# RMSNorm and matmul on one core: the stores of tiles 0 and 1 divided into eleven transfers each

## The chip, the cores and the metric

The kernel runs on one core of one Trainium2 chip. The metric is the device time of one execution in microseconds (us); lower is better. The kernel before takes 209.87 us, the median of three runs (209.15 to 210.03). A profile is one execution recorded by the hardware profiler. In it PE is TensorE's matmul, PEld its weight load, DVE VectorE, ACT ScalarE, POOL GpSimd and SP SyncE, which computes nothing and only issues transfers. Sixteen DMA engines move the data; a transfer (one `dma_start`) is cut into packets that are spread over them, and each engine that takes part reports its part's end to a semaphore.

## The reference

```python
# x: 16 x 1024 x 512, gamma: 512, weight: 512 x 768, all float32; eps = 1e-5
rms = np.sqrt(np.mean(x ** 2, axis=-1, keepdims=True) + eps)
x_norm = x / rms * gamma
return np.matmul(x_norm, weight).astype(np.float32)
```

There are 16,384 tokens. The input x is 33.6 MB and the output 50.3 MB; with the weights of 1.6 MB all of it crosses between HBM and the core's memory once.

## The kernel before, in words

**Tiles.** A tile is 128 tokens, one on each partition; there are 128 tiles, worked on in pairs (2j, 2j+1). For each tile ACT squares and sums the 512 features (`square`, L205), and from the sums come the root (L210, ACT) and its reciprocal `rstd` (L212, DVE). POOL casts x to bf16 (`cast`, L188). TensorE turns the tile so that features lie on partitions (`transpose_word`, L239; DVE copies the result from PSUM, L248). One quad of tiles in sixteen is cast at L269 and turned by DVE instead (L280). TensorE then multiplies by the weights, which gamma has already scaled: four weight loads (L305) and eight products (L309) per tile into one of three accumulators. `finish_tile` scales the accumulator by `rstd` and writes it to the output tile `ot`: even tiles by ACT (L288), odd tiles by DVE (L290). Then it calls `store`.

**Loads.** `load` (L177) brings x in stretches of 4 tiles (twice) and then of 8. Those of tiles 0 to 31 and the two halves of the weights (L354) are issued by SP at the very start; later ones by ACT, each when the loop reaches a set pair (`load_until`). Gamma (L349) is the first transfer of all: two rows of 1024 bytes, issued by ACT.

**Stores.** `store` (L297 to L302) does nothing until the last tile of a stretch is written, and then issues one transfer for the whole stretch on SP. The stretches (`o_first`, `o_size`, L138) are 1, 1, 2 and 4 tiles in the first group, 8 tiles in each of the middle groups, and 4, 4, 4, 2, 2 at the end: 22 stores. The output tiles lie in three buffers of 8 tiles; group g writes buffer g % 3. So tiles 24 to 31 write the buffer from which tiles 0 to 7 were stored, and have to wait until those stores have landed. In general, ACT's and DVE's writes of group g wait for the stores of group g - 3.

**Rows.** `rows` (L140) says which rows of x or of the output belong to a tile. In the first eight tiles, a stretch of 4 tiles takes 512 tokens in a row, and partition p holds tokens 4p to 4p + 3. The store of tile 0 alone (or of tile 1 alone) therefore writes 128 separate rows of 768 floats, 3072 bytes each. A store of 8 tiles writes 24,576 bytes together from each partition.

**Order.** Nothing is scheduled by a planner. The code calls `run` and `order.transfer` in the order that is wanted, and `Order.emit` (L39 to L97) issues the instructions to each engine in that order. It finds from the cells that each step reads and writes which earlier steps it has to wait for, and puts those waits ahead of it on its engine. A transfer is a step of its own with its own semaphore, or one whose last transfer is known to be done; whoever waits for a transfer waits for that semaphore. An engine runs its instructions in order, so a wait holds up all that is queued behind it on that engine. SP's queue has, in order: the early loads, and then the 22 stores.

Of the kernel before, what the change touches and what calls it, by code (L numbers as in the profile page):

```python
# [16 lines left out]
P = 128  # L17
# [83 lines left out]
def kernel(  # L101
# [9 lines left out]
    PE, DVE, ACT, POOL, SP = nc.tensor, nc.vector, nc.scalar, nc.gpsimd, nc.sync  # L111
    order = Order(tc)
# [5 lines left out]
    out = out.flatten_outer_dims()  # L118
# [5 lines left out]
    XG, OG = 16, 8  # L124
# [15 lines left out]
    def rows(ap, i, n):  # L140
        base, t = (i - i % OG, OG) if OG <= i < XG else (x_first[i], x_size[i]) if i < OG else (i - i % XG, XG) if i < 2 * XG else (i - i % (2 * XG), 2 * XG)
        return ap[base * P:(base + t) * P, :].rearrange("(p t) d -> p t d", t=t)[:, i - base:i - base + n, :]

    def sb(name, shape, dtype):
        return nc.alloc_sbuf_tensor(name, shape, dtype).ap()
# [14 lines left out]
    ot = [sb(f"ot{n}", [P, OG, O], F32) for n in range(3)]  # L160
# [7 lines left out]
    def cells(name, slot, i, n=1):  # L168
        return [(name, slot, t) for t in range(i, i + n)]
# [124 lines left out]
    def accumulator():  # L294
        return next(turns) % 3

    def store(i):  # L297
        first, n = o_first[i], o_size[i]
        s = first // OG % 3
        if i == first + n - 1:  # L300
            src = ot[s][:, first % OG:first % OG + n, :]
            order.transfer(SP, lambda: SP.dma_start(out=rows(out, first, n), in_=src), reads=cells("ot", s, first % OG, n))  # L302

    def hold(lhsT, of):
        run(PE, lambda: PE.ldweights(lhsT), of)  # L305
# [20 lines left out]
    def finish_tile(i, a, engine):  # L326
        s = i // OG % 3

        before = [("ot", s, i % OG - 1)] if i == o_first[i] + o_size[i] - 1 else []
        scale(engine, ot[s][:, i % OG, :], ops[a][:, :O], rstd[:, i:i + 1],  # L330
              [("ops", a, 0), ("ops", a, 1), ("rstd", i)] + before, [("ot", s, i % OG)])
        store(i)
# [158 lines left out]
```

## Time and profile before

| | |
|---|---|
| median of three runs | 209.87 us (209.15 to 210.03) |
| profiled execution: its own time | 208.59 us |
| its span (first to last instruction) | 206.6 us |
| busy in the span | PE 193.4, PEld 72.6, DVE 149.5, ACT 144.3, POOL 59.9 us |
| moved | 85.62 MB in 5920 packets, mean 414 GB/s |
| the two stores of 384 KB | 20.5 us from issue to landing (median) |
| DMA packets under 512 bytes | 658 |

How to read it: the span is less than the time of the execution, since the time holds what lies before the first and after the last instruction. Busy times say how long each engine was at work, not what the end waited for. That is read from the chain of waits (followed back from the last instruction to whatever released it), from stages of the span (busy time and DMA share in each) and from the landings of transfers. A DMA share of 1.00 means that all sixteen engines were moving packets all of the time. A transfer's time to landing counts from its issue, so it holds the time that it stood in line behind others.

### The profile page before, as it was taken

The numbers are of one execution on the slowest core, as the hardware profiler recorded it, in microseconds if no ns is written. First come the engines' busy times: TensorE is split into PE (matmuls) and PEld (weight loads), VectorE is DVE, ScalarE is ACT, GpSimd is POOL, SyncE is SP. The second block draws the span as 40 slices with busy tenths as digits, with TensorE's granted clock in tenths as the row PEclk, the third lists the DMA queues.
The fourth block names the chain that finished last, engine by engine and source line by source line (L and its number), as shares of the span: only waits on it lengthen the run. The fifth ranks groups of instructions, "written<-read, shape, count | busy, mean of one in ns | idle before, by whom it ended". The sixth has DMA issues, their size and how long they took to land.

```text
span 206.6 us, 2755 instructions
## 1 busy us (share of the span) xinstructions
PE 193.4 (94%) x1212; PEld 72.6 (35%) x717; DVE 149.5 (72%) x255; ACT 144.3 (70%) x343; POOL 59.9 (29%) x34
## 2 busy tenths in 40 slices
PE   6699999999999999999999999999999999999940
PEld 0134444433334333433333333433344324343310
DVE  0446556999579975999569974999569974999530
ACT  2698998777777687677877687676948758683310
POOL 1436752067005250063304242060703307000000
PEclk9799999999999999999999999999999999999995
DMA  5999999999999999999999999999999999999993
GB/s 207 428 444 425 412 388 423 423 441 425 433 428 425 428 438 427 424 430 425 431 438 425 425 433 417 443 424 424 428 425 438 433 428 428 436 424 405 416 418 165
DMA packets 5920, 85.62 MB, mean 414 GB/s; under 512 B 658, under 2 KB 660, under 8 KB 1556
## 3 DMA queue, kind: packets, MB, share of 16 engines
q1 hardware_dynamic: 4176, 60.29, 69.0%
q10 hardware_dynamic: 1732, 25.17, 28.7%
q8 instruction: 7, 0.11, 0.2%
q14 instruction: 5, 0.04, 0.0%
HBM read 35.13 MB, written 50.33 MB: 414 GB/s over the span
## 4 chain that ended last, share of the span: by engine, by line
PE 75%; DMA 15%; DVE 5%; issue 1%; ACT 1%; SPq 0%; ACTq 0%
PE ps L309 66%; DMA out_dram<-ot 12%; PE ps L239 9%; DMA xt<-in_x_dram 2%; DVE ot L290 2%; DVE xT L248 1%; DVE xTq L280 1%; ACT ot L288 0%; ACT jk L205 0%; DVE w_bf L290 0%; DVE rstd L212 0%; ACT rms L210 0%; SPq L486 0%; ACTq L93 0%; SPq L445 0%
## 5 line engine op out<-in xcount | busy, mean ns | idle before, releaser
L309 PE MATMUL ps<-w_bf,xT 128*128 128x256 bf16 (+1 forms) x783 | 145.7, 326 | 1.8 <-DVE w_bf L290 0.5
L288 ACT ACTIVATE ot<-ps,rstd 128x768 f32<-128x768 f32 x64 | 57.5, 898 | 47.4 <-PE ps L309 38.0
L188 POOL CAST xb<-xt 128x2048 bf16<-128x2048 f32 (+3 forms) x21 | 46.4, 2218 | 113.3 <-PE ps L239 57.4
L205 ACT ACTIVATE w_f<-xt 128x512 bf16<-128x512 f32 x124 | 76.3, 619 | 0.1
L290 DVE TENSOR_SCALAR ot<-ps,rstd 128x768 f32<-128x768 f32 x64 | 64.8, 1013 | 10.3 <-PE ps L309 9.3
L305 PEld LDWEIGHTS <-xT 128*128 128x128 bf16 x400 | 39.4, 98 | 60.4 <-issue 59.1
L239 PE MATMUL ps<-ident_f,xb 128*128 128x128 f32 x200 | 54.0, 273 | 1.7 <-POOL xb L188 1.6
L248 DVE COPY xT<-ps 128x1024 bf16<-128x1024 bf16 (+1 forms) x53 | 34.6, 654 | 24.3 <-PE ps L239 23.7
L280 DVE STREAM_TRANSPOSE xTq<-xq 32x256 f32<-32x256 f32 x112 | 48.7, 435 | 1.9
L239 PEld LDWEIGHTS ps<-ident_f,xb 128*128 128x128 f32 x200 | 28.1, 141 | 46.6 <-issue 43.8
L309 PE MATMUL ps<-w_bf,xTq 128*128 128x256 bf16 (+1 forms) x217 | 41.8, 324 | 0.4
L205 ACT ACTIVATION_READ_ACCUMULATOR w_f<-xt 128x1 f32 x124 | 23.6, 191 | 0.0
L305 PEld LDWEIGHTS <-xTq 128*128 128x128 bf16 x112 | 11.0, 98 | 14.5 <-issue 14.5
L269 POOL CAST xq<-xt 128x2048 bf16<-128x2048 f32 x7 | 13.3, 1893 | 0.0
L212 DVE RECIPROCAL rstd<-rms 128x8 f32<-128x8 f32 (+3 forms) x20 | 3.9, 193 | 8.9 <-ACT rms L210 8.7
L210 ACT ACTIVATE rms<-ssq,eps_sb 128x8 f32<-128x8 f32 (+3 forms) x20 | 6.0, 300 | 0.7
L309 PE MATMUL ps<-warm 128*128 128x512 bf16 x10 | 4.3, 568 | 1.4 <-DVE eps_sb L363 1.4
L205 ACT ACTIVATE jk<-xt 128x512 bf16<-128x512 f32 x4 | 2.5, 618 | 3.1 <-DMA xt<-in_x_dram 3.1
L288 ACT ACTIVATE w_bf<-w_f,g_sb 128x768 bf16<-128x768 f32 x2 | 1.9, 936 | 1.1 <-DMA w_f<-in_weight_dram 1.1
L386 DVE COPY g_sb<-ps 128x4 f32<-128x4 f32 x1 | 0.2, 161 | 3.1 <-PE ps L380 3.1
L350 ACT ACT_TABLE_LOAD x1 | 1.3, 1283 | 1.5 <-SPq L445 1.5
L290 DVE TENSOR_SCALAR w_bf<-w_f,g_sb 128x512 bf16<-128x512 f32 (+2 forms) x3 | 1.4, 481 | 0.6 <-DMA w_f<-in_weight_dram 0.6
(12 smaller groups left out, 3.0 us busy)
## 6 DMA issues: line engine op xcount, KB each, us to landing
out_dram<-ot SPq DMA_DIRECT2D x13, 3072.0 KB, 22.6
xt<-in_x_dram ACTq DMA_DIRECT2D x12, 2048.0 KB, 19.5
xt<-in_x_dram SPq DMA_DIRECT2D x3, 2048.0 KB, 17.7
out_dram<-ot SPq DMA_DIRECT2D x4, 1536.0 KB, 10.8
out_dram<-ot SPq DMA_DIRECT2D x3, 768.0 KB, 6.7
xt<-in_x_dram SPq DMA_DIRECT2D x2, 1024.0 KB, 6.9
w_f<-in_weight_dram SPq DMA_DIRECT2D x2, 768.0 KB, 7.1
out_dram<-ot SPq DMA_DIRECT2D x2, 384.0 KB, 20.5
```

Of the source, the lines that this page charges most:

```text
L188: run(POOL, lambda: POOL.tensor_copy(out=xb[s][:, i % 8:i % 8 + n, :], in_=src), of, cells("xb", s, i % 8, n))
L205: run(ACT, lambda: ACT.activation(out=dst, in_=src[:, 0, :], func=AF.Square, accum_out=ssq[:, i:i + 1]), of, to + [("ssq", i)])
L210: run(ACT, lambda: ACT.activation(out=rms[:, s], in_=ssq[:, s], func=AF.Sqrt, scale=1.0 / D, bias=eps_sb), [("ssq", t) for t in range(i, i ...
L212: run(DVE, lambda: DVE.reciprocal(out=rstd[:, s], in_=rms[:, s]), [("rms", i)], [("rstd", t) for t in range(i, i + n)])
L239: run(PE, lambda: PE.transpose(out=tp[b][:, t, h, :], in_=words[:, lo:lo + P], identity=ident_f), cells("xb", s, j % 4 * 2 + t) + ["ident" ...
L248: run(DVE, lambda: DVE.tensor_copy(out=dst[:, t:t + n, :], in_=src[:, t:t + n, :]), [("tp", b)], cells("xT", j % 4, t, n))
L269: run(POOL, lambda: POOL.tensor_copy(out=xq[s], in_=src), of, [("xq", s)])
L280: run(DVE, lambda: DVE.transpose(out=dst, in_=src), [("xq", s)], [("xTq", s, n)])
L288: run(ACT, lambda: ACT.mul(out=dst, in_=src, mul=r), reads, writes)
L290: run(DVE, lambda: DVE.tensor_single_scalar(out=dst, in_=src, scalar=r, op=mybir.AluOpType.mult), reads, writes)
L305: run(PE, lambda: PE.ldweights(lhsT), of)
L309: run(PE, lambda: PE.add_instruction(mybir.InstMatmult(name=nc.get_next_instruction_name(), engine=mybir.EngineType.PE, ins=[PE.lower_ap(r ...
```

## The change

The stores of tiles 0 and 1 are no longer one transfer each but eleven, all issued by SP, one after the other. Together they write the same 128 rows to the same places. The parts are cut by partition:

- eight transfers of seven rows: partitions 0, 4, ..., 24; then 1, 5, ..., 25; 2, ..., 26; 3, ..., 27; and the same four from 32 on (32, 36, ..., 56 and so on)
- one transfer of 64 rows: partitions 64 to 127
- two transfers of four rows: partitions 28 to 31, and 60 to 63

All other stores stay as they were. SP issues 42 stores in place of 22. Each of the new transfers has a semaphore, so ACT, before it writes tile 24, waits for eleven transfers of tile 0 instead of one, and DVE before tile 25 for eleven of tile 1. The order of the instructions on all engines but SP is unchanged.

```diff
+    DIVIDED = (0, 1)
+    PARTS = [slice(lo + m, lo + 28, 4) for lo in (0, 32) for m in range(4)] + [slice(64, P), slice(28, 32), slice(60, 64)]
+
     def store(i):
         first, n = o_first[i], o_size[i]
         s = first // OG % 3
         if i == first + n - 1:
-            src = ot[s][:, first % OG:first % OG + n, :]
-            order.transfer(SP, lambda: SP.dma_start(out=rows(out, first, n), in_=src), reads=cells("ot", s, first % OG, n))
+            src, dst = ot[s][:, first % OG:first % OG + n, :], rows(out, first, n)
+            for part in PARTS if first in DIVIDED else [slice(0, P)]:
+                store_rows(dst[part], src[part], cells("ot", s, first % OG, n))
+
+    def store_rows(dst, src, of):
+        order.transfer(SP, lambda: SP.dma_start(out=dst, in_=src), reads=of)
```

## The prediction

> **What bounds the kernel now.** I read the page first (engine and DMA rows in 40 slices), then stages, then the chain that ended last, then the stores, and last the packet and landing records of the trace.
>
> From the page, the slices (tenths busy, one column per 5.2 us):
>
> ```profile
> PE   6699999999999999999999999999999999999940
> ...
> DMA  5999999999999999999999999999999999999993
> GB/s 207 428 444 425 412 388 423 423 441 425 433 428 425 428 438 427 424 430 425 431 438 425 425 433 417 443 424 424 428 425 438 433 428 428 436 424 405 416 418 165
> ```
>
> TensorE and the sixteen DMA engines are both full from the third slice to the last but two. The stages part them (time in each stage, PE busy and instructions, then PEld, DVE, ACT, POOL, granted clock, DMA share, GB/s):
>
> ```profile
> 26.00:44.00 18.00, 17.89 (x119) 7.26 (x72) 13.47 (x23) 15.49 (x40) 6.91 (x3) 1.00 1.02 424
> 44.00:80.00 36.00, 35.74 (x230) 13.40 (x133) 29.15 (x49) 27.11 (x67) 11.48 (x6) 1.00 1.00 427
> ...
> 160.00:180.00 20.00, 19.42 (x125) 7.20 (x72) 15.25 (x27) 14.77 (x36) 5.51 (x3) 1.00 1.01 430
> 180.00:190.00 10.00, 9.95 (x66) 3.86 (x39) 9.65 (x18) 5.75 (x13) 0.00 (x0) 1.00 0.98 420
> 190.00:200.00 10.00, 8.60 (x53) 2.48 (x26) 5.67 (x8) 3.19 (x4) 0.00 (x0) 1.00 0.98 414
> 200.00:207.00 7.00, 0.00 (x0) 0.00 (x0) 0.00 (x0) 0.00 (x0) 0.00 (x0) 0.65 0.50 206
> ```
>
> From 44 us on the DMA share is 0.98 to 1.01 while TensorE already rests 1.40 us in 190:200. So the end belongs to transfers. The chain, its last long piece and who waits for a store:
>
> ```profile
> 142.42 25.11 DMA out_dram<-ot
> 167.62 0.91 ACT ot L288
> ...
> 198.69 1.02 DVE ot L290
> ```
>
> ```profile
> L302 SPq DMA_DIRECT2D out_dram<-ot x22: 332/332/348, 13.0 to 200.0; - x22
> ...
>   ACT ot L288: 9.2, 4
>   DVE ot L290: 0.4, 1
> ...
> DMA to landing us min/median/max: 5.7/22.0/25.4
> ```
>
> The last store is issued at 200.00 and lands 5.7 us later. The chain calls all that one DMA, but the landing records split it: each engine reports its own sixteenth. These are the sixteen landings of the last store (us), then the latest landing of each of the last six stores:
>
> ```
> 203.22 203.28 203.30 203.31 203.31 203.39 203.40 203.46 203.73 203.94 203.96 204.00 204.66 204.72 205.06 205.66
> 190.71 194.47 198.22 201.96 203.81 205.66
> ```
>
> The latest engine moves 98 KB (its part of 1536 KB) in 3.75 us and 49 KB in 1.85 us, back to back, to the end: it never runs dry, and its backlog, not the last tile, ends the kernel. Eight engines are through by 203.46, 2.20 us sooner. Every store before the change gives each engine the same bytes, so the lag comes from elsewhere: instruction packets (seven of 16 KB, near 1 us each), and slow packets (of the 1527 packets of 24576 bytes after 56 us, 1384 took 911 to 916 ns, and about a hundred 922 to 962). A change of the bytes per engine therefore moves the end one for one, if it touches the last engine.
>
> **The change part by part.** A tile's store is 128 rows of 3072 bytes: 16 engines with 8 rows each (the two stores left 256 packets of that size). A seven-row transfer can occupy at most seven engines, a four-row one four; 64 rows give four to each of sixteen. The nearest row for a short transfer is the gamma load: two rows, two packets, started 1 ns apart on two engines. Which engines the seven are, no row tells. One end: a different set each time, then the load stays near eight rows and nothing moves. Other end: always the same seven, and the four-row ones the first four of them. I take the second, since the five 128-row transfers of the first 22 us landed with the same spacing each time (0 to 0.46 us): the assignment is fixed, not turning. Then per tile four engines carry 8+4+2 = 14 rows, three 8+4 = 12, nine 4 in place of 8.
>
> The Trainium skill, DMA: Bandwidth & Descriptors (Why a DMA increments its semaphore by 16 and not by 1), states the same split: the largest count up to 16 that divides the rows, on the lowest-numbered engines; no run here shows the numbers.
>
> Prices: a 3072-byte packet took 121 ns (median of 256, mean 122, longest 229), a semaphore packet 9 ns. Over both tiles:
> - four engines: 12 x 121 + 20 more semaphore packets x 9 = +1.63 us
> - three engines: 8 x 121 + 16 x 9 = +1.11 us
> - nine engines: -8 x 121 = -0.97 us (none above -8 x 229 = -1.83).
>
> Issue on SP: 20 more at 0.33 us is 6.6 us (at most 1.25 us each, the longest issue of this trace, which is 25). The first store was issued at 12.95, the second at 14.49, the store of tiles 2 and 3 at 17.35, the next at 24.54. With the change the second starts near 16.8 and tiles 2 and 3 near 20.6, 3.2 us late. All is hidden: the same queue still holds x loads, and the first 3072-byte packet moved only at 26.05. If that cover went, the store of tiles 8 to 15 (36.36) would come late next. No load is queued behind on SP: later x loads are issued by ACT.
>
> Waits: ACT waits for eleven transfers instead of one before it writes tile 24, DVE the same before tile 25; queued behind are the squares of later tiles (ACT), and on DVE the transposes that TensorE's products need. The tiles' stores landed by 41.01, ACT writes tile 24 at 48.49, so with 1.63 us more they are still there; what is left is ten passed waits. None below zero; above, ten times the shortest short instructions (ACT's accumulator read, 191 ns) is 1.9 us on each. I take zero, because ACT sat idle 0.70 us for TensorE before that tile and 0.48 before the next, and DVE's queue is 29.15 of 36 us busy; a rest would eat TensorE's lead over the transfers (1.40 us idle in 190:200), not the end.
>
> Sum: the latest engine, if one of the nine, ends at 205.66 - 0.97 = 204.69; the other late ones likewise at 204.09 or before. The four heavier ones, if among the first twelve, end at 203.22 + 1.63 = 204.85 to 204.00 + 1.63 = 205.63. The end is the later: between 204.69 and 205.63, so -0.97 to -0.03; I take the middle of where the eight early ones put it (203.46 + 1.63 = 205.09) and a little above, 205.2, so -0.45 us. The profiled execution took 208.59 (span 206.6 and 2.0 around it), 1.28 under the median of the runs and under the fastest of them; the sum gives 208.14 for it and 209.87 - 0.45 = 209.4 for the median.
>
> Nine in sixteen engines being relieved, a late engine is one of them with 0.56 by count. Seven engines began their x packets early (1.96 to 2.04 us; one of gamma's two among them, the other one held by gamma to 2.97), eight late (2.69 to 2.83). As far as chains of packets, each starting where one ended, can be followed, six of the early seven are through by 203.6; if the short transfers sit on gamma's side, they load early engines, so I go to 0.65. The Trainium skill (same page, Latency and other measured facts) calls engines 7 and 15 usually the slower ones; by it the last engine is relieved here. No run here shows which number it has.
>
> **Rivals.**
> 1. Slower: a heavier engine was already late. From a landing later than 205.66 - 1.63 = 204.03 the load makes the end worse: 204.66 gives +0.63, 205.06 gives +1.03, 205.66 gives +1.63 (three engines' share: +1.11). For it: four landings lie above 204.03, and by count alone one of the four heavier engines is likelier than not to have one of them. Against: the early start group above. 210.5 to 211.5; +1.05 is passed only by the last engine itself or by the waits on top.
> 2. Slower: transfers of one row per engine cost more than their bytes. For it: in 26:35, where the two small stores moved, the rate was 410 GB/s against 427 in 44:80, 4% of 9 us, 0.36 us; eleven times the transfers gives up to 3.9 us, 213.8. It decides from (1.05 + 0.45) / 20 = 75 ns per extra transfer. Against: two 768 KB stores at the end took 2 x 1.85 us where one of 1536 KB took 3.75, so an additional boundary cost nothing. The Trainium skill (same page, Rules for kernel authors) says transfers under 64 KB pay mostly overhead, and these have 21 and 12 KB; no row here has such a store.
> 3. Same: the seven turn round the engines, or the heavier ones reach just the old end: 209.87.
> 4. Faster: the relieved engine gains more than its rows' median (up to 1.83 us, 208.0), and the heavier engines were idle at the end, waiting for the store issued at 200.00, so that their load costs less. For it: the early eight land together, as engines do that wait for an issue. Against: mean packet 122 ns.
>
> **How the numbers follow.** About 0.5% (1.05 us) is what a measurement here can tell from no change. Forecast 0.52, all of it within 0.5% (-0.97 to 0; its own range 208.9 to 209.9). Rival 1: 0.24, of it 0.16 slower by over 0.5%, 0.08 within. Rival 2: 0.12, slower. Rival 3: 0.03, within. Rival 4: 0.09, faster. Faster 0.09, same 0.63, slower 0.28. The range goes from 208.7 (a part of rival 4) to 211.5 (all of rival 1) and leaves out rival 2 and most of rival 4, under 0.2.
>
> **What would show it.** The landings of the small stores: seven-row ones with seven late parts. In the last store, the spread from first to last landing (2.44 us) shrinks to about 1.5 with the last one near 205.2. The chain still ends with the last store, issued within 0.3 us of 200.00. Rate in the slice around 26 to 35 us shows rival 2: a fall well under 410 GB/s. Wrong, if the spread grows (rival 1), if TensorE's busy share falls in the stage 44:80 (waits), or if the last store's fastest part lands clearly later than 203.22.

## The result, and the profile after

The changed kernel takes 211.14 us (median of six runs, 210.65 to 211.38). Beside it the kernel before took 209.81 us. The ratio is 1.0086, with a 95% interval of 1.006 to 1.0112: slower by 0.9%, where -0.2% was forecast. The ratio and its interval are formed from undisturbed executions alone, and are not the quotient of the two medians, which is 1.0063. 211.14 lies within the stated range, on its wrong side.

The profiled execution took 210.70 us with a span of 208.6, against 208.59 and 206.6. The page of the changed kernel, slices of 5.2 us (line numbers of the changed file are 7 higher behind the store: L316 is L309 of before, L309 is L302):

```profile
PE   7799999999999999998998989999898999999980
DMA  5999999999999999999999999999999999799886
GB/s 220 420 441 440 390 383 418 427 447 413 438 423 432 441 416 438 412 434 427 429 435 424 435 427 429 416 421 430 434 435 421 435 424 443 324 415 415 337 343 286
```

Before, the DMA row stood at 9 up to the last slice. Now the transfers thin out in the last sixth, and TensorE has gaps in the middle instead. The stages say the same:

```profile
44.00:80.00 36.00, 36.00 (x235) 13.42 (x134) 29.05 (x48) 26.86 (x65) 11.24 (x6) 1.00 1.01 430
80.00:120.00 40.00, 38.71 (x252) 14.77 (x146) 32.21 (x55) 28.14 (x68) 10.93 (x4) 1.00 1.01 430
120.00:160.00 40.00, 38.19 (x246) 14.22 (x141) 28.70 (x48) 26.04 (x63) 11.06 (x5) 1.00 1.00 426
160.00:180.00 20.00, 19.11 (x124) 7.07 (x71) 15.69 (x27) 16.35 (x39) 7.33 (x3) 1.00 1.01 431
180.00:190.00 10.00, 10.00 (x68) 4.04 (x40) 9.57 (x18) 7.44 (x20) 0.00 (x0) 1.00 0.88 374
190.00:200.00 10.00, 10.00 (x65) 3.24 (x33) 7.65 (x12) 3.61 (x4) 0.00 (x0) 1.00 0.79 332
```

TensorE rests 1.29 + 1.81 + 0.89 us in the stages from 80 to 180, in all 4.0; before it was 0.26 + 0.26 + 0.58 = 1.1 (39.74 of 40 twice, 19.42 of 20). After 180 TensorE is full, and the DMA share falls to 0.79. The kernel before ended on transfers with TensorE at rest; this one ends on TensorE with engines of the DMA at rest. What TensorE waited for is told by the list of waits (us in all, times, longest), before and after; then come the store's view and the chain from 90 us on, both after:

```profile
ACT ot L288 <- DMA out_dram<-ot: 9.2, 4, 2.7
...
DVE ot L290 <- DMA out_dram<-ot: 0.4, 1, 0.4
PE ps L309 <- ACT ot L288: 0.4, 1, 0.4
```

```profile
ACT ot L288 <- DMA out_dram<-ot: 22.5, 8, 3.9
...
DVE ot L290 <- DMA out_dram<-ot: 4.5, 6, 1.1
PE ps L316 <- ACT ot L288: 4.0, 6, 0.9
```

```profile
L309 SPq DMA_DIRECT2D out_dram<-ot x42: 280/412/912, 12.9 to 204.1; - x42
...
  ACT ot L288: 22.5, 8
  DVE ot L290: 4.5, 6
...
DMA to landing us min/median/max: 3.4/19.1/27.0
```

```profile
95.34 27.04 DMA out_dram<-ot
122.46 0.91 ACT ot L288
...
132.30 27.88 DMA out_dram<-ot
160.27 0.91 ACT ot L288
...
202.83 1.02 DVE ot L290
```

ACT and DVE waited 27.0 us for stores to free `ot`, where they had waited 9.6. While ACT waits, it does not empty the accumulator that TensorE needs next: TensorE waited 4.0 us for those writes of ACT, where it had waited 0.4, and 4.0 is also what it rests between 80 and 180. Two stores of the middle are now links of the chain, with 27.04 and 27.88 us from issue to landing (the second is not among those that the store's view times), where one was before, with 25.11. The last store is issued at 204.14 us instead of 200.00, and lands in 3.4 us instead of 5.7: its sixteen parts land between 207.36 and 207.54, so no engine has a backlog any more. So 4.1 us later at the issue, 2.3 us less behind it, 1.9 us later at the end.

Which engines were late can be read in this trace, because the new stores mark the engines: of a tile, one with 14 rows moves ten in short transfers, one with 12 eight, one with 4 none. Followed in chains (each packet begins where one ended), four engines had the first pattern, three the second, nine the third. How late each landed its part of a middle store, near 103 us, behind the earliest engine (us):

```
four engines of 14 rows    2.94  3.09  3.76  6.65
three engines of 12 rows   2.41  3.02  3.99
nine engines of 4 rows     0.00  0.07  0.15  0.31  0.54  1.02  1.40  1.51  1.62
```

By this reading all seven are behind all nine. One chain among the four is far behind the others; it also took three 8 KB instruction packets, at 29, 89 and 158 us. The chain with the slow packets (28 ns over the usual 912) is one of the three. Chains can be mixed up where two packets end together, so what single chains say beyond the pattern at the start is a reading, not a proof. It needs no chains to see that the load landed on the latest engine: the store of tiles 8 to 15, the first of a whole group behind the two tiles, has its first part at 54.50 us, where it was 54.91, and its last at 59.54, where it was 57.78. So the earliest part came 0.4 us sooner and the latest 1.8 us later.

Only the stores fell behind, not the loads of x. The store issued at 82.96 us landed at 110.00, but the load that ACT issued at 88.88, 5.9 us after it, was complete at 108.06; before, the two landed in the order of their issue (106.27 and 109.37). From first to last part the loads of this stretch took 2.9 to 3.6 us, against 2.4 to 4.0 before. What a late engine owes stands in the queue of the stores, and loads pass it.

### The profile page after: what moved, and what is told of

It is laid out like the page before. It is cut to its first block, busy times and chain, and to the rows that moved or that the text cites. A ratio compares the mean times of both kernels' runs of the same rounds, so it can differ in the third digit from the quotient of the medians.

```text
span 208.6 us, 2809 instructions
## 1 busy us (share of the span) xinstructions
PE 196.1 (94%) x1236; PEld 72.8 (35%) x717; DVE 149.7 (72%) x255; ACT 143.8 (69%) x343; POOL 59.9 (29%) x34
## 4 chain that ended last, share of the span: by engine, by line
PE 61%; DMA 29%; DVE 5%; ACT 1%; issue 1%; SPq 0%; ACTq 0%
PE ps L316 54%; DMA out_dram<-ot 26%; PE ps L239 7%; DVE ot L290 2%; DMA xt<-in_x_dram 2%; DVE xT L248 1%; DVE xTq L280 1%; ACT ot L288 1%; ACT jk L205 0%; DVE w_bf L290 0%; DVE rstd L212 0%; ACT rms L210 0%; ACTq L93 0%; SPq L493 0%; SPq L452 0%
## 5 line engine op out<-in xcount | busy, mean ns | idle before, releaser
L316 PE MATMUL ps<-w_bf,xT 128*128 128x512 bf16 (+1 forms) x800 | 149.0, 327 | 4.2 <-ACT ot L288 4.0
L316 PE MATMUL ps<-w_bf,xTq 128*128 128x512 bf16 x224 | 42.8, 326 | 0.0
L316 PE MATMUL ps<-warm 128*128 128x512 bf16 x10 | 4.8, 629 | 1.4 <-DVE eps_sb L370 1.4
```

The costliest lines, as they stand in the source:

```text
L316: run(PE, lambda: PE.add_instruction(mybir.InstMatmult(name=nc.get_next_instruction_name(), engine=mybir.EngineType.PE, ins=[PE.lower_ap(r ...
```

## The experiments

Two theories at the outset. **Load**: seven engines get more bytes, are later for the rest of the run, and their late landings hold up the writes of `ot`. **Transfers**: twenty more transfers cost something each, on the engines, on SP, or by the waits of ACT and DVE. All runs below were timed in four groups, each beside the kernel before, at 209.0 to 209.2 us.

### Equal load, many transfers (even16)

```diff
-    PARTS = [slice(lo + m, lo + 28, 4) for lo in (0, 32) for m in range(4)] + [slice(64, P), slice(28, 32), slice(60, 64)]
+    PARTS = [slice(lo, lo + 16) for lo in range(0, P, 16)]
```

> Each of the two stores in eight transfers of 16 consecutive rows, one row per engine: many short transfers, but each engine keeps its eight rows per tile. Theory L (load: the first seven engines get more bytes, are late for the rest of the run, and the late landings hold up ACT's and DVE's writes of ot): no change from before, 209.8 us, within 0.4. Theory T (the number of transfers: each extra one costs its engines or SP something beyond its rows; 20 extra ones cost 1.33 us, so 0.067 each): 14 extra give at least +0.9, 210.7.

Measured: 209.34 us beside 209.0, ratio 1.0012 (0.9997 to 1.0027). Fourteen more transfers cost nothing that can be told from zero, where the theory of the transfers wanted 0.9 us.

### The same unequal load, fewer transfers (five)

```diff
+    PARTS = [slice(0, 49), slice(49, 56), slice(56, 120), slice(120, 124), slice(124, P)]
```

> Each of the two stores in five transfers of 49, 7, 64, 4 and 4 rows: seven engines with 7 rows, seven with one, sixteen with four, four with one and four with one, so 14, 12 and 4 rows per tile as in the changed kernel, with 8 extra transfers in place of 20 and SP through sooner. Theory L: as the changed kernel, 211.1 us, within 0.4. Theory T: 8 x 0.067 = +0.5, 210.3.

Measured: 210.76 us, ratio 1.0096 (1.0059 to 1.0132), as much as the changed kernel, with eight extra transfers in place of twenty. The theory of the transfers gave +0.5 us, 0.24%, which the interval excludes; with even16 it falls. The stage from 80 to 160 us of before, even16, five and the changed kernel (PE busy stands first behind the length), each in its own fence:

```profile
80.00:160.00 80.00, 79.48 (x512) 30.61 (x303) 65.18 (x110) 59.13 (x143) 23.82 (x10) 1.00 1.01 429
```

```profile
80.00:160.00 80.00, 79.28 (x510) 30.35 (x302) 64.82 (x110) 58.83 (x142) 23.86 (x10) 1.00 1.01 430
```

```profile
80.00:160.00 80.00, 76.53 (x486) 29.05 (x288) 61.83 (x103) 55.16 (x133) 22.01 (x9) 1.00 1.01 429
```

```profile
80.00:160.00 80.00, 76.89 (x496) 28.99 (x287) 60.92 (x102) 54.18 (x131) 21.99 (x9) 1.00 1.01 428
```

TensorE rests 0.5 and 0.7 us with equal loads, 3.5 and 3.1 with unequal ones, while the DMA share is the same 1.00 to 1.01: the engines are all busy, but not on what is waited for.

### Which engines: low4, half, six, fives, low4s, low2

These six move the load about. Rows per tile on each engine; largest lag (how far the last part of a store landed behind its first, the worst of the nine or ten stores that land from 50 to 170 us); what TensorE waited in all for ACT's writes of `ot`; and the ratio. Lag and wait are those of the one profiled execution:

```
            rows on the engines                    largest lag   wait   ratio (95%)
before      8 on all                                   3.3 us     0.4 us
even16      8 on all                                   3.1        0.9   1.0012 (0.9997 to 1.0027)
low4        14 on the first four, 6 on twelve          5.1        1.0   1.0011 (0.999  to 1.0032)
half        14, 12 and 4, but tile 0 alone             5.7        1.9   1.0056 (1.0025 to 1.0087)
fives       15 on four, 13 on the fifth, 5 on eleven   6.4        1.8   1.0073 (1.0048 to 1.0098)
low2        15 on two, 7 on fourteen                   6.4        2.0   1.0026 (1.0008 to 1.0044)
six         13 on the first six, 5 on ten              6.8        2.5   1.0072 (1.0046 to 1.0098)
five        14 on four, 12 on three, 4 on nine         7.8        3.0   1.0096 (1.0059 to 1.0132)
after       14 on four, 12 on three, 4 on nine         8.7        4.0   1.0086 (1.006  to 1.0112)
low4s       17 on the first four, 5 on twelve          9.0        3.2   1.0121 (1.0077 to 1.0166)
```

Each is an edit of the same line, `PARTS` (or `DIVIDED`):

```diff
+    PARTS = [slice(0, 96)] + [slice(lo, lo + 4) for lo in range(96, P, 4)]                              # low4
+    DIVIDED = (0,)                                                                                      # half
+    PARTS = [slice(0, 80)] + [slice(lo, lo + 6) for lo in range(80, P, 6)]                              # six
+    PARTS = [slice(0, 80)] + [slice(lo, lo + 5) for lo in range(80, 120, 5)] + [slice(120, 124), slice(124, P)]   # fives
+    PARTS = [slice(0, 80)] + [slice(lo, lo + 4) for lo in range(80, P, 4)]                              # low4s
+    PARTS = [slice(0, 112)] + [slice(lo, lo + 2) for lo in range(112, P, 2)]                            # low2
```

> Each of the two stores in nine transfers: 96 rows (six per engine) and eight of four rows. The first four engines carry 14 rows per tile as in the changed kernel, the other twelve 6. Theory L with the late engine among the first four (one of them lands its part of the middle stores up to 8.6 us after the earliest engine): as the changed kernel or a little less, 210.7 to 211.3. Theory L with the late engine among the next three (where the slow packets of 940 ns are): these are now relieved by two rows per tile, 209.4 to 209.9. Theory T: 16 x 0.067 = +1.1, 210.9, which this run does not part from the first.

> Only tile 0's store is divided into the eleven; tile 1's is one transfer. Half the extra load and half the transfers. Both theories give a part: theory T 10 x 0.067 = +0.67, 210.5. Theory L: the waits for ot grow with the lag of the latest engine, the first part of the lag is still covered by the buffers: less than half, 209.9 to 210.5.

low4 cost nothing, although its first four engines carry as much as in the changed kernel; so the next three, or the deeper relief of the other nine (4 rows, not 6), have a part in the cost. half came out at 0.56%, above half of the whole: the expectation of a small first part is not borne out, though its interval reaches down to 0.25%.

> Each of the two stores in nine transfers: 80 rows (five per engine) and eight of six rows. The first six engines carry 13 rows per tile (+5), the other ten 5 (-3), counted as the short transfers fill the engines from the first. The engine that decides is one of the fifth to seventh (low4 loaded the first four by +6 and cost nothing measurable). If it is the seventh: it is relieved by 3 rows per tile, 0.7 us over both; no slower than before, 208.4 to 209.3 beside 209.0. If it is the fifth or sixth: it gets +5 rows per tile, 1.2 us, and with 13 rows about what it has in the changed kernel (12): +0.6 to +1.0%, 210.3 to 211.1.

> Each of the two stores in eleven transfers: 80 rows (five per engine), eight of five rows and two of four. The first four engines carry 15 rows per tile, the fifth 13, the other eleven 5. If the late engine is the fifth: as six, +0.6 to +1.0%. If it is the sixth or seventh: it is relieved by 3 rows per tile, and the first four are at +7, one more than in low4, which cost nothing measurable: 208.6 to 209.8 beside 209.0.

Both are slower by 0.7%, which pointed to the fifth engine as the one that decides. The next two runs were made to break that.

> Each of the two stores in thirteen transfers: 80 rows (five per engine) and twelve of four. The first four engines carry 17 rows per tile (+9, more than in any run so far), the other twelve 5 (-3). Theory F5 (the fifth engine decides: it is the one that fives and six load and low4 relieves): it is relieved, so no slower than before, 208.6 to 209.6. Theory F4 (any engine decides once its parts of the middle stores land more than some 5 us after the earliest; low4 with 14 rows was just under that, 5.1 us and +0.11%, fives with 15 just over, 6.4 us and +0.73%): the latest landing is 6.5 to 7.5 us after the first, and the time is +0.8 to +1.3%, 210.6 to 211.7.

> Each of the two stores in nine transfers: 112 rows (seven per engine) and eight of two. Two engines carry 15 rows per tile (+7), fourteen 7 (-1). Theory F5: 208.6 to 209.6. Theory F4: +7 is what fives gives the first four; if one of the two is an engine that is late by itself, as in fives, +0.5 to +0.9%; if neither is, their lag is the +7 rows alone, under 5 us, and the time is that of before.

low4s relieves the fifth engine and has the largest ratio of all, 1.2%, though its interval overlaps those of five and the changed kernel. The theory of one deciding engine falls. The first four alone will do, if they get enough: at 14 rows they are still covered (5.1 us, +0.1%), at 17 they are not (9.0 us, where 6.5 to 7.5 was expected, and +1.2%); and where the engines behind them are loaded too, 13 to 15 rows already cost 0.7 to 1.0%. The ratio goes roughly with the largest lag and with TensorE's wait: nothing that can be told from zero up to 5.1 us and 1.0 us, and more above. A slope can't be drawn from this: each lag is that of one execution, low4's the fastest of its twelve (208.45 us, median 209.42), low4s's 0.9 us under its median.

low2 is out of line, and neither of its expectations came true: its lag was 6.4 us, not under 5, and its cost +0.26%, not 0.5 to 0.9%. Its profiled execution was a usual one (209.66 us, median 209.67). Loaded and relieved engines differ by the same eight rows in low2, low4 and six, for 0.26, 0.11 and 0.72%, so neither the bytes nor the worst lag alone give the time. With two engines late, less may be held up; that was not tried, and which single engines are late by themselves stays open.

### The load at the end instead of the beginning (late5, late5e)

```diff
+    DIVIDED = (124,)
+    PARTS = [slice(0, 49), slice(49, 56), slice(56, 120), slice(120, 124), slice(124, P)]              # late5
+    PARTS = [slice(0, 64), slice(64, 80), slice(80, 96), slice(96, 112), slice(112, P)]                # late5e, the control
```

> Tiles 0 and 1 are stored as before; the store of tiles 124 and 125, the last but one, is divided as in the run five (49, 7, 64, 4 and 4 rows of 6144 bytes, 234 ns each): the first four engines get 6 more rows, 1.4 us, the next three 4 more, 0.94 us, nine 4 fewer, 0.94 us. The same load as in the changed kernel, but after all waits for ot. If the late engines are late through the run and the load adds to their backlog: the last store's latest part lands 0.9 to 1.4 us later and the time is +0.4 to +0.7%, 209.9 to 210.5 beside 209.0, with ACT's wait for stores at the 9 us of before. If load only counts early, through the waits for ot: no change, within 0.3.

> The control: the same store in five transfers of 64, 16, 16, 16 and 16 rows, equal bytes on all engines. Only the four extra transfers at the end are left: SP issues them in 0.35 us each while the last store is due 2.9 us later, so no change, 208.8 to 209.3 beside 209.0; if short transfers at the end cost by themselves, as much as late5.

Measured: late5 210.21 us, 1.0052 (1.0016 to 1.0089); late5e 209.53, 1.0007 (0.9982 to 1.0032). The median of late5 is as expected; that of late5e lies 0.2 us above its range, with a ratio of no change. But the intervals overlap, and the profiles spoil the test: with little queued, each of the five issues took SP 0.35 to 1.46 us, the last store was issued only at 203.35 (late5) and 203.41 (late5e), and so most of the backlog was waited out on SP. It agrees with the theory of the load, and settles little.

### Slack in the middle (slack_before, slack_after)

```diff
         while starts and starts[0] < i:
-            load(starts.pop(0))
+            n = starts.pop(0)
+            if n not in (32, 40):
+                load(n)
```

> The kernel before without the loads of tiles 32 to 39 and 40 to 47 (they are computed from the x of tiles 0 to 15, still in the buffer, so their output is not the reference's): 4.2 MB less, some 10 us of the sixteen engines' time between 24 and 60 us, in which a late engine can catch up. Faster than before, as the waits for ot (9.6 us in all) and the backlog at the end go: TensorE's own time, 204 to 208 us beside 209.0. It is here for the comparison with the next.

> The changed kernel without the same two loads. If the unequal load costs because no engine ever catches up while the queues are full (theory of this study): the 2 to 3 us that it makes are drained in the slack, and the time is that of the run beside it within 0.3%, with like waits for ot. If the change costs through something else that stays (SP's later issues, the eleven waits on ACT and DVE, the transfers themselves): +0.9% over the run beside it, as with the full loads.

Measured, both against the full kernel before: 0.9855 (0.9827 to 0.9882) and 0.9854 (0.9829 to 0.9878). With 10 us of slack for the engines early on, the change costs nothing that can be told from zero. The unequal bytes, the 42 issues on SP and the eleven waits are all still there. The stage from 80 to 160 us, slack_before and slack_after:

```profile
80.00:160.00 80.00, 79.47 (x512) 30.58 (x303) 65.41 (x110) 60.02 (x143) 24.50 (x10) 1.00 1.00 427
```

```profile
80.00:160.00 80.00, 79.47 (x512) 30.52 (x303) 65.14 (x110) 59.80 (x143) 24.24 (x10) 1.00 1.00 425
```

TensorE rests 0.53 us in both, and in neither does any instruction wait for a store: the rows "ACT ot" and "DVE ot" of the store's view are gone. The largest lags of the stores are alike, 4.2 and 4.4 us. By itself this pair would leave open whether the bytes or the number of transfers took the engines' time, since slack hides both; even16 and five settle that. Together the four runs show the cause: extra bytes on some engines cost as long as the queues are so full that these engines never catch up.

## Why the prediction was wrong, point by point

**What bounds the kernel** was read half. Rightly, the latest engine never ran dry and its backlog ended the kernel before. But "a change of the bytes per engine therefore moves the end one for one, if it touches the last engine" left out the second way to the end: a late engine also lands the middle stores late, and ACT and DVE wait for those. The 9.6 us of such waits stood in the prediction's own lines. As they were, TensorE waited 0.4 us for ACT because of them; with 27.0 us of them it is 4.0. The sign of it that the prediction named, a fall of TensorE's busy share in 44:80, did not come (36.00 of 36 us, 35.74 before): the fall is in the stages behind, from 80 to 180.

**The failed step** is the place of the late engines: "a late engine is one of them with 0.56 by count", raised to 0.65 by the chains. With the latest engine among the relieved nine, the last landing would have come 0.03 to 0.97 us sooner, by the prediction's sum. In the changed kernel the last part of the store of tiles 8 to 15 landed 1.8 us later, about the +1.63 of the four heavier engines with nothing taken off; and by the chains the seven loaded engines are all behind the nine relieved ones, the one with slow packets among them. So the -0.97 us on the nine was worth nothing, and the +1.63 and +1.11 on the seven counted. Which engines were late before the change was read from chains that can be mixed up; no run settles it engine by engine. The Trainium skill (DMA: Bandwidth & Descriptors, Latency and other measured facts) calls engines 7 and 15 usually the slower ones, and puts that, as a guess, down to transfers that GpSimd issues. SP and ACT issue all transfers here, and no trace numbers its engines, so that sentence gave no ground for taking the last engine as a relieved one.

**The step that followed from it** is "I take zero" for the waits. It held for tiles 24 and 25, the only writes that it looked at, and not for the groups behind them. The lead of TensorE that was to absorb a rest was 1.40 us; TensorE waited 3.6 us more for ACT.

**The split** into 14, 12 and 4 rows, the step no row told, was right, and the landings show it. The eight seven-row transfers of tile 0 landed one behind the other, some 0.19 us apart (last parts at 27.24, 27.43, 27.62 us and so on), as parts do that queue on the same seven engines. Of the 64-row transfer, nine parts landed by 28.65 and seven from 29.06 to 30.46. Of the first seven-row transfer of tile 1, three parts landed by 30.98 and four only from 33.66 on, behind the four-row transfers of tile 0.

**Rival 1** happened. Its 210.5 to 211.5 us hold the measured 211.14, and its +1.63 us lies between the measured +1.3 (the medians) and +1.8 (0.86% of 209.8). That is luck, since its path was another: a backlog at the end, shown by a growing spread in the last store. The spread went from 2.44 to 0.18 us. The compute had been held up in the middle, so that the last store was issued 4.1 us later and found no backlog.

**Rival 2** (short transfers cost more than their bytes) is excluded as the main cost by even16, with sixteen such transfers at +0.12% (at most 0.27%), and by five, with fewer transfers at the full cost. Its sign, a fall of the rate in 26:35, did come: 391 GB/s, where it was 410. In even16 the rate was 408, in five 403, so it does not go with the time either.

**SP's issues** were priced too low: 0.33 us taken, 0.70 measured for a seven-row transfer (1.25 was the bound). Tiles 2 and 3 were issued at 27.89 us, 10.5 late, not 3.2. It stayed hidden, as foreseen: five has issued all its parts by 17.1 us and costs the same.

**The eleven waits** were rightly costed at nothing. ACT's write of tile 24 before, and then after the change:

```profile
48.48 0.90 ACT L288 ACTIVATE ot<-ps,rstd 128x768 f32<-128x768 f32 x1 [0.69 <-PE ps L309]
```

```profile
48.24 0.90 ACT L288 ACTIVATE ot<-ps,rstd 128x768 f32<-128x768 f32 x1 [0.70 <-PE ps L316]
```

Both wait 0.7 us for TensorE, and no longer. The parts of tiles 0 and 1 had landed by 40.97 us; before, it was 35.04 (the prediction's 41.01 is the store of tiles 2 and 3).

## What to carry to other kernels

While the transfer queues never run dry, an engine that falls behind with the stores stays behind: 25 to 37 KB more on seven of sixteen engines at 30 us cost 0.9% at 210 us, and the same bytes cost nothing where 10 us of slack followed. So cut transfers such that every engine gets the same bytes; how many transfers that takes matters little (sixteen in place of two: +0.1%). Read the spread of one store's landings, not only its last, and ask of it twice: does the last part end the kernel, and who waits for the last parts in the middle?

## What was not expected of the hardware

- SP took 0.70 us to issue seven rows that lie four partitions apart, 0.33 for a store of 128 rows, and about 0.35 from one issue to the next for four or five adjacent rows.
- The lag of the latest engine grew along the run, in the changed kernel from 5.0 us at 55 to 8.7 at 151, with equal bytes for all engines in that stretch; in the kernel before it stayed at 2.9 (3.3 at most), and in low4 at 4.6 (4.0 to 5.1). In five, six, half and low4s it grew too, by 2 to 3 us. Slow packets and instruction packets may account for a part; why it grows in some and not in others was not settled.
- The loads of x, issued by ACT, landed on time while the stores, issued by SP, were up to 8.7 us apart on the same sixteen engines.
- Leaving out 4.2 MB of loads, 5% of the bytes, gave only 1.45%: TensorE is close behind the transfers.
